# Eight attention heads beside a projection: the norm weights of queries and keys, four short steps and the score products change place and engine

## The chip, the cores and the metric

The kernel runs on one core of one Trainium2 chip. The metric is device time in microseconds of one execution, lower is better. The time given for a kernel is the median of its runs, and beside it stands one further execution that was profiled.

## What is computed

One layer of a streaming encoder, for 512 new frames of a prompt and 64 frames that continue a running stream with 512 cached positions (together 576 columns, called T in the kernel). All arithmetic is in float32. The part that matters here is the attention of eight heads:

```python
hn = rmsnorm(x, g_norm1)
proj = hn @ w_in                                     # 576 x 2048 by 2048 x 6144
q = rmsnorm(q.reshape(B, T, N_HEADS, HEAD_DIM), g_q) # per head, 128 wide
k = rmsnorm(k.reshape(B, T, N_HEADS, HEAD_DIM), g_k) # k, with g_k, is an output too
z = einsum(q, k) / sqrt(HEAD_DIM)                    # scores
log_1mb = where(mask, log_sigmoid(-z), 0)
after = reversed cumulative sum of log_1mb over keys, without the key itself
w = where(mask, exp(log_sigmoid(z) + after), 0)
o_attn = w @ v
```

Around it stand a short gated convolution, an output projection, and a feed-forward block, which the change leaves as they are.

## The kernel before

**Precision.** A float32 matrix is split into a high part in a reduced format and a low part (the rest), and a product is three matmuls: high by high, low by high, high by low. The high part is a copy on ScalarE (`cast`, L728; for weights L206), the low part a subtraction on VectorE (`low`, L731; for weights L209). Three subtractions of a head run on GpSimd instead (`low_pool`, L742): `s1l`, `s0l` and `vl`.

**Stages.** The program first loads and turns x, then runs some projections as block products ("units", PE line L1038, until about 162 us of the profile), then the last twelve column blocks of the input projection one after the other (PE line L247, tile `pj`; called the late projection here), then the convolution, the output projection and the feed-forward block (L1389, L1901). The attention of the eight heads is woven into the late projection and the first of the convolution, from about 163 to 441 us.

**What sets the order.** A small class `Pipeline` counts ticks. One tick is one step of a product, three matmuls of `pj`. `attend(h)` is a generator; it says `yield until(n)` to be called again n ticks after its start, and head h starts 49 ticks after head h-1. Whatever it issues then goes, in that order, into the queues of all engines. In this stage TensorE (PE), VectorE (DVE), ScalarE (ACT), GpSimd (POOL) and the DMA queue of SyncE (SP) all keep the program's order, so an instruction that waits holds up all that stands behind it on its engine. A head takes 104 ticks and the next starts after 49: two heads are always under way, and what I call the *frame* of head h (ticks counted from its start) also holds the second half of head h-1.

**One head, in ticks of its frame (before).** At 0 the raw queries and keys (`Eq`, `Ek`) and the cached keys `cK` are loaded; at 9 and 11 ScalarE squares them (L778) and at 12 VectorE sums the squares (L781). At 18 PE adds the sums over partitions (`ss`, L788), and ScalarE and VectorE make the factor 1/rms from them (L790 to L797). At 21 VectorE multiplies keys, then queries, by that factor, and GpSimd multiplies each by its norm weights (L800, L801). At 25 and 27 VectorE turns them into `kf` and `qf` (L804, L807), ScalarE makes the high parts `kh`, `qh`, VectorE the low parts `kl`, `ql` (28 and 30). The finished keys go out to HBM at 28 (`put_tokens`, eight DMAs, L716). From 36 to 41 PE computes the scores `z` (L832, L835). ScalarE and VectorE make softplus values `pr`, their high and low parts `ph` and `pl`, and the sums `s1`, `s0`. At 60, 63 and 66 PE adds the cumulative sums into `z` (L893 to L912), after each VectorE limits it (L883) and ScalarE takes the exponent (L885) and the high part again. At 67 and 69 the values get their parts `vh`, `vl`. At 78 PE multiplies weights and values (`po`, L937, L940). From 70 on the same follows for the 64 columns of the running stream (`sp`, `cz` at 87, `os` at 99).

**Weights.** Each block of weights (1 MB) has one place in memory: its two ScalarE copies stand 7 ticks after the start of each block of 32 ticks, its two VectorE subtractions `wlo` at 9 and 11, and the load of the block after it at 16, which waits for these subtractions. So these fall at another place of the frame in each head: in the frames of heads 1, 3 and 5 both subtractions stand between `ss` and the scores.

Of the kernel before, what the change touches and what calls it, by code (L numbers as in the profile page):

```python
# [16 lines left out]
P = 128  # L17
# [81 lines left out]
def tile_hybrid_stream_step(  # L99
# [26 lines left out]
    small = rpad.tile([P, 88], F32, name="rpad_t")  # L126
    NB = T // 32
    eps_r, gk_t, quad = small[:, :NB], small[:, NB : NB + 32], small[:, NB + 32 : NB + 36]
    gq_t = small[:, 56:88]
# [179 lines left out]
    def load_vectors():  # L309
        r0 = 0  # L310
        for name, ap, n in (("gq", g_q[0], 1), ("gk", g_k[0], 1),
                            ("ga", g_attn_out[0], NH), ("gc", g_conv_out[0], NG),
                            ("cw", conv_w[0].rearrange("w d -> (w d)"), 3 * NG),
                            ("st", state_conv[0, 0].rearrange("w d -> (w d)"), 2 * NG), ("g2", g_norm2[0], KD)):
            rows[name] = r0
            nc.sync.dma_start(out=vraw[r0 : r0 + n, :], in_=ap.rearrange("(r c) -> r c", c=P))
            r0 += n
        for q in range(4):
            nc.sync.dma_start(out=gk_t[32 * q : 32 * (q + 1), :],
                              in_=g_k[0, 32 * q : 32 * (q + 1)].partition_broadcast(32))  # L320
            nc.sync.dma_start(out=gq_t[32 * q : 32 * (q + 1), :],
                              in_=g_q[0, 32 * q : 32 * (q + 1)].partition_broadcast(32))

    g1c = const.tile([P, KD], F32, name="g1c")
    vec = const.tile([P, P], F32, name="vec")

    def turn_vectors():
# [3 lines left out]
        nc.vector.tensor_scalar(out=gq_t, in0=gq_t, scalar1=1.0 / math.sqrt(P), scalar2=None, op0=ALU.mult)  # L331
# [7 lines left out]
    def col(name, i=0):  # L339
        return vec[:, rows[name] + i : rows[name] + i + 1]  # L340
# [386 lines left out]
    def cast(hi, src):  # L727
        nc.scalar.copy(out=hi, in_=src)  # L728
# [12 lines left out]
    def low_pool(lo, src, hi):  # L741
        nc.gpsimd.tensor_tensor(out=lo, in0=src, in1=hi.bitcast(F32), op=ALU.subtract)  # L742

    late_E = {}

    def attend(h):
        clock = [0]

        def until(t):
            d, clock[0] = t - clock[0], t  # L750
            assert d >= 0
            return d
# [4 lines left out]
        for n, c in (("q", 0), ("k", 1)):  # L757
            if (c, h) in late_E:
                E[n] = late_E[c, h]
            else:  # L760
                E[n] = t1.tile([P, T], F32, tag="E" + n, name="E" + n)
                nc.sync.dma_start(out=E[n], in_=qk_dram[2 * h + c])
        cK = t1.tile([P, TP], F32, tag="cK", name="cK")
# [3 lines left out]

        def chunks(t, w=32):
            return t.rearrange("p (b c) -> p b c", c=w)

# [8 lines left out]
        yield until(12)  # L779
# [6 lines left out]
        yield until(18)  # L786
# [7 lines left out]
        yield until(21)  # L794
# [3 lines left out]
        for i, (n, g) in enumerate((("k", gk_t), ("q", gq_t))):  # L798
            r = ms[:, NB * (1 - i) : NB * (2 - i)].unsqueeze(2).to_broadcast([P, NB, 32])
            nc.vector.tensor_tensor(out=chunks(E[n]), in0=chunks(E[n]), in1=r, op=ALU.mult)  # L800
            nc.gpsimd.tensor_tensor(out=chunks(E[n]), in0=chunks(E[n]),  # L801
                                    in1=g.unsqueeze(1).to_broadcast([P, NB, 32]), op=ALU.mult)
            yield until(23 + 2 * i)
        nc.vector.transpose(out=kf, in_=E["k"])  # L804
        cast(kh, kf[:, : 3 * P])
        yield until(27)
        nc.vector.transpose(out=qf, in_=E["q"])  # L807
# [32 lines left out]
        yield until(38)  # L840
        scores(1)
        soft_log(pr[1], z[1][:, :384])
        yield until(39)
# [3 lines left out]
        yield until(41)  # L847
# [5 lines left out]
        yield until(43)  # L853
# [6 lines left out]
        yield until(44)  # L860
# [3 lines left out]
        yield until(46)  # L864
# [5 lines left out]
        yield until(48)  # L870
        low_pool(s1l, pb[2], s1h)
        cast(s0h, pb[1])
        yield until(50)
        cast(ph[0], pb[0])
        low_pool(s0l, pb[1], s0h)
        if h != 7:
            load_values(h)
        yield until(52)
# [9 lines left out]
        yield until(56)  # L888
        if h == 7:
            load_values(h)  # L890
        vtok = vtoks.pop(h)
        yield until(60)
# [5 lines left out]
        yield until(63)  # L898
# [5 lines left out]
        yield until(64)  # L904
# [3 lines left out]
        yield until(66)  # L908
# [5 lines left out]
        yield until(67)  # L914
# [4 lines left out]
        yield until(69)  # L919
        low_pool(vl, vtok[:, 0:3, :], vh)  # L920
# [3 lines left out]
        yield until(70)  # L924
        sp = scratch[:, 1280 : 1280 + T]
        soft_log(sp[:, :320], zc)
        yield until(73)
# [7 lines left out]
        yield until(78)  # L935
# [5 lines left out]
        yield until(79)  # L941
# [4 lines left out]
        yield until(81)  # L946
# [3 lines left out]
        yield until(87)  # L950
# [8 lines left out]
        yield until(88)  # L959
        nc.scalar.activation(out=ws[:, TS:], in_=ws[:, TS:], func=AF.Exp)  # L960
        yield until(99)
# [5 lines left out]
        for i, (a, b) in enumerate(HALVES):  # L967
            yield until(101 + 2 * i)
            add_squares(acc_a[:, a:b], o_attn[h][:, a:b], h == 0, scratch[:, HALF * i : HALF * (i + 1)])
# [195 lines left out]
    for q in (2, 3):  # L1165
        pipe.spawn(unit_prepare(*horder[q]))
# [1084 lines left out]
```

## Time and profile before

| | us |
|---|---|
| median of 3 runs (lowest, highest) | 2370.11 (2366.62, 2373.37) |
| the profiled execution, its own time | 2372.08 |
| its span, first to last instruction | 2370.3 |
| PE busy | 2334.1 |
| DVE busy | 1907.4 |
| ACT busy | 1150.0 |
| POOL busy | 315.0 |

The profiled execution lies 2.0 us above the median and inside the three runs. In rows of the profile, `out<-in` are the tiles that an instruction writes and reads, and "idle before" is the time that its engine stood still just before it, with the instruction whose end released it. A granted clock (PEclk) of 0.50 means that TensorE ran at half rate in that stretch.

### The profile page before, as it was taken

To read this page: it belongs to the slowest core of one execution; us is meant where nothing else is said; L and a number is where in the kernel's file an instruction comes from. 1 tells how busy PE (TensorE), PEld (TensorE's weight loads), DVE (VectorE), ACT (ScalarE), POOL (GpSimd) and SP (SyncE) were. 2 spreads that over 40 slices of the span, in tenths; PEclk is the share of its full clock that TensorE was granted. 3 is DMA by queue.
4 is the path that set the end of the run, shared out by engine and by line. 5 is a ranking of instruction groups with operands and counts; after the bars stand their busy time and mean duration, and the time that the engine had idled before them with its cause. 6 is when DMAs were issued, how large, how long until landed. Compare 5 with 4: busy or idle time off the path is not lost.

```text
span 2370.3 us, 43741 instructions
## 1 busy us (share of the span) xinstructions
PE 2334.1 (98%) x17461; PEld 2320.3 (98%) x17461; DVE 1907.4 (80%) x2817; ACT 1150.0 (49%) x1994; POOL 315.0 (13%) x424
## 2 busy tenths in 40 slices
PE   8999999999999999999999999999999999999999
PEld 8998898999999999999999999999999999999998
DVE  8876667688887889888888888888888777887886
ACT  7536666444444555444444444444444444444444
POOL 2003544212111220000000000000000001431121
PEclk9999999999999999999999999999999999999999
DMA  8785455784468655554554554554554946885654
GB/s 274 200 226 136 114 125 116 231 271 120 125 213 238 180 160 167 147 144 134 147 146 133 147 147 133 146 148 132 146 149 133 339 133 197 228 236 190 197 127 105
DMA packets 584836, 401.97 MB, mean 170 GB/s; under 512 B 92030, under 2 KB 572024, under 8 KB 584632
## 3 DMA queue, kind: packets, MB, share of 16 engines
q1 hardware_dynamic: 573704, 378.03, 54.6%
q0 software_dynamic: 10064, 20.65, 3.9%
q8 instruction: 137, 2.24, 0.4%
q10 hardware_dynamic: 864, 0.49, 0.1%
q14 instruction: 67, 0.55, 0.1%
HBM read 303.25 MB, written 95.86 MB: 168 GB/s over the span
## 4 chain that ended last, share of the span: by engine, by line
PE 79%; DVE 8%; DMA 5%; issue 3%; ACT 2%; SPq 1%; POOL 1%; DVEq 0%; ACTq 0%; POOLq 0%
PE psy L1901 34%; PE psw L1901 17%; PE psx L1901 8%; PE psy L1389 6%; PE pj L247 3%; PE psw L1389 3%; PE psy L1038 2%; DMA raw_a<-in_w_in_dram 2%; PE psx L1389 1%; PE psw L1038 1%; DMA Eq<-qk_dram 1%; DVE wlo L209 1%; DMA raw_a<-in_w_down_dram 1%; PE psx L1038 1%; PE pjo L247 1%
## 5 line engine op out<-in xcount | busy, mean ns | idle before, releaser
L1901 PE MATMUL psy<-h_s,whl 128*128 128x288 f32 x2787 | 411.6, 295 | 0.8 <-DMA h_s<-hid_dram 0.6
L1901 PEld LDWEIGHTS psy<-h_s,whl 128*128 128x128 f32 x2787 | 383.4, 188 | 1.3 <-DMA h_s<-hid_dram 0.8
L257 DVE TENSOR_TENSOR whl<-raw_a,whl 128x1024 fp32r<-128x1024 f32 (+4 forms) x296 | 316.8, 1071 | 60.1 <-ACT whl L256 58.9
L1901 PE MATMUL psw<-t,whl 128*128 128x288 f32 x2400 | 347.2, 295 | 0.0
L1901 PEld LDWEIGHTS psw<-t,whl 128*128 128x128 f32 x2400 | 327.3, 188 | 0.3 <-DVE whl L257 0.2
L256 ACT CAST whl<-raw_a 128x1024 fp32r<-128x1024 f32 (+4 forms) x296 | 268.1, 907 | 108.4 <-issue 35.4
L247 PE MATMUL pj<-x,whi 128*128 128x288 f32 x1376 | 298.0, 301 | 0.4 <-DVE x L408 0.2
L257 DVE TENSOR_TENSOR whl<-raw_b,whl 128x1024 fp32r<-128x1024 f32 (+5 forms) x190 | 197.5, 1040 | 69.4 <-ACT whl L256 68.2
L256 ACT CAST whl<-raw_b 128x1024 fp32r<-128x1024 f32 (+5 forms) x190 | 165.0, 871 | 168.9 <-issue 73.0
L1911 ACT COPY part<-psy 128x288 f32<-128x288 f32 x242 | 96.4, 398 | 279.5 <-PE psy L1901 276.7
L247 PEld LDWEIGHTS pj<-x,whi 128*128 128x128 f32 x1376 | 229.9, 191 | 2.1 <-DVE x L408 1.1
L247 PE MATMUL pj<-x,wlo 128*128 128x288 f32 x688 | 204.8, 298 | 0.1
L1901 PE MATMUL psy<-t2t,whl 128*128 128x288 f32 x1212 | 183.7, 295 | 0.0
L1901 PE MATMUL psy<-b22m,whl 128*128 128x288 f32 x1212 | 183.3, 295 | 0.0
L1901 PE MATMUL psx<-h_s,whl 128*128 128x288 f32 x1185 | 173.6, 295 | 0.0
L1901 PEld LDWEIGHTS psy<-t2t,whl 128*128 128x128 f32 x1212 | 168.3, 188 | 0.2 <-DVE whl L257 0.2
L1901 PEld LDWEIGHTS psy<-b22m,whl 128*128 128x128 f32 x1212 | 168.0, 188 | 0.0
L1901 PEld LDWEIGHTS psx<-h_s,whl 128*128 128x128 f32 x1185 | 162.3, 188 | 0.0
L247 PEld LDWEIGHTS pj<-x,wlo 128*128 128x128 f32 x688 | 132.2, 192 | 1.1 <-DVE wlo L475 0.3
L1680 POOL DMA_DIRECT2D hid_dram<-form x3 | 2.3, 755 | 970.4 <-DVE form L257 970.4
L256 ACT CAST whl<-s 128x1024 fp32r<-128x1024 f32 (+5 forms) x81 | 72.2, 892 | 99.9 <-PE psw L1901 99.8
L1901 PE MATMUL psy<-t,whl 128*128 128x288 f32 x576 | 107.5, 296 | 1.9 <-ACT part L1911 1.9
(534 smaller groups left out, 4527.0 us busy)
## 6 DMA issues: line engine op xcount, KB each, us to landing
hid_dram<-form SPq DMA_DIRECT2D x147, 288.0 KB, 2.6
raw_a<-in_w_in_dram SPq DMA_DIRECT2D x33, 1024.0 KB, 6.1
raw_a<-in_w_gate_dram SPq DMA_DIRECT2D x22, 1024.0 KB, 5.8
raw_a<-in_w_up_dram SPq DMA_DIRECT2D x22, 1024.0 KB, 5.8
raw_b<-in_w_gate_dram SPq DMA_DIRECT2D x22, 1024.0 KB, 8.3
raw_b<-in_w_up_dram SPq DMA_DIRECT2D x22, 1024.0 KB, 7.3
h_s<-hid_dram SPq DMA_DIRECT2D x10, 2016.0 KB, 12.8
raw_a<-in_w_out_dram SPq DMA_DIRECT2D x16, 1024.0 KB, 5.8
```

Source lines behind the costliest of these rows:

```text
L209: nc.vector.tensor_tensor(out=lo[:, a : a + 1024], in0=raw[:, a : a + 1024], in1=hi[:, a : a + 1024].bitcast(F32), op=ALU.subtract)
L247: mm(ps, w_[:, k, csl], x_, start=(k == 0 and n == 0), stop=(k == nk - 1 and n == 2))
L256: nc.scalar.copy(out=hi, in_=src)
L257: (lo_eng or nc.vector).tensor_tensor(out=lo, in0=src, in1=hi.bitcast(F32), op=ALU.subtract)
L1038: mm(ps, whl[:, w_, j, :], x_, start=(start and j == 0 and q == 0), stop=(j == NP - 1 and q == 2), skip_group_check=True)
L1389: mm(ps, whl[:, w_, j, :], x_, start=(start and j == 0 and q == 0), stop=(j == m - 1 and q == 2), skip_group_check=True)
L1680: q.dma_start(out=hid_dram[fp][2 * n - 2 : 2 * n].rearrange("f p t -> p f t"), in_=t.bitcast(F32))
L1901: mm(ps, whl[:, w_, j, :], x_, start=(start and j == 0 and q == 0), stop=(j == len(xs_) - 1 and q == 2), skip_group_check=True)
L1911: nc.scalar.copy(out=t, in_=st["y"])
```

## The change

For each head:

- The norm weights are multiplied in after the turn, by ScalarE, as the per-partition scale of a copy in place: `gqs` (query weights by 1/sqrt(128)) for `qf`, the column of `g_k` for `kf`, 128x576 each. GpSimd's two multiplications before the turn go; one of them comes back behind the turn of the keys, for the key output alone.
- VectorE now takes queries first, then keys, and turns each right after its product with 1/rms.
- `s1l`, `s0l` and `vl` are subtracted on VectorE; `low_pool` is gone.
- Later ticks: `cK` is loaded at 6 instead of 0, the sums stand at 13 (12), `ss` at 20 (18), the key output at 35 (28), the scores at 46 (36), and all behind them ten ticks later, but for `cz`, which is eleven later. The head's last step is at 113.
- Head 7 loads its values like the others, at 60.
- Outside the heads, the fourth preparation of unit weights starts 3 ticks after the third instead of with it, and the broadcast copy of `g_q` with its four DMAs is gone.

```diff
-        yield until(18)
+        yield until(20)
         ss = misc("ss")[:, : 2 * NB]
         mm(ss, same, sums, start=True, stop=True)
...
-        for i, (n, g) in enumerate((("k", gk_t), ("q", gq_t))):
-            r = ms[:, NB * (1 - i) : NB * (2 - i)].unsqueeze(2).to_broadcast([P, NB, 32])
+        for i, n in enumerate("qk"):
+            r = ms[:, NB * i : NB * (i + 1)].unsqueeze(2).to_broadcast([P, NB, 32])
             nc.vector.tensor_tensor(out=chunks(E[n]), in0=chunks(E[n]), in1=r, op=ALU.mult)
-            nc.gpsimd.tensor_tensor(out=chunks(E[n]), in0=chunks(E[n]),
-                                    in1=g.unsqueeze(1).to_broadcast([P, NB, 32]), op=ALU.mult)
-            yield until(23 + 2 * i)
-        nc.vector.transpose(out=kf, in_=E["k"])
+            yield until(25 + 2 * i)
+            nc.vector.transpose(out=f[n], in_=E[n])
+        nc.gpsimd.tensor_tensor(out=chunks(E["k"]), in0=chunks(E["k"]),
+                                in1=gk_t.unsqueeze(1).to_broadcast([P, NB, 32]), op=ALU.mult)
+        yield until(28)
+        nc.scalar.activation(out=qf, in_=qf, func=AF.Copy, scale=gqs)
+        cast(qh, qf[:, :TP])
+        yield until(30)
+        nc.scalar.activation(out=kf, in_=kf, func=AF.Copy, scale=col("gk"))
         cast(kh, kf[:, : 3 * P])
-        yield until(27)
-        nc.vector.transpose(out=qf, in_=E["q"])
-        cast(qh, qf[:, :TP])
-        yield until(28)
+        yield until(31)
+        low(ql, qf[:, :TP], qh)
+        yield until(33)
         low(kl, kf[:, : 3 * P], kh)
+        yield until(35)
+        nc.vector.transpose(out=cK, in_=cK)
         put_tokens(E["k"], kp[:, h, :], 0, TP)
         put_tokens(E["k"], ks[:, h, :], TP, T)
-        yield until(30)
-        low(ql, qf[:, :TP], qh)
-        yield until(31)
-        nc.vector.transpose(out=cK, in_=cK)
-        yield until(36)
+        yield until(46)
...
-        low_pool(s1l, pb[2], s1h)
+        low(s1l, pb[2], s1h)
...
-        low_pool(s0l, pb[1], s0h)
+        low(s0l, pb[1], s0h)
...
-        low_pool(vl, vtok[:, 0:3, :], vh)
+        low(vl, vtok[:, 0:3, :], vh)
...
-        pipe.spawn(unit_prepare(*horder[q]))
+        pipe.spawn(unit_prepare(*horder[q]), 3 * (q - 2))
```

VectorE in the frame of head 3, between the factor 1/rms and the scores, before. `wlo` are the weight subtractions, `z`, `pl`, `vl` belong to head 2, the rest to head 3; `raw_a` 128x36 is the factor.

```order
L796 TENSOR_TENSOR raw_a<-raw_a 128x36
L797 SCALAR_TENSOR_TENSOR raw_a<-raw_a 128x36
L800 TENSOR_TENSOR Ek<-Ek,raw_a 128x576
L209 TENSOR_TENSOR wlo_3214<-raw_a,whi_3213 128x1024
L800 TENSOR_TENSOR Eq<-Eq,raw_a 128x576
L739 SCALAR_TENSOR_TENSOR raw_a<-raw_a 128x320
L209 TENSOR_TENSOR wlo_3214<-raw_a,whi_3213 128x1024
L804 STREAM_TRANSPOSE kf<-Ek 128x576
L807 STREAM_TRANSPOSE qf<-Eq 128x576
L731 TENSOR_TENSOR kl<-kf,kh 128x384
L1120 STREAM_TRANSPOSE El<-pj 128x288
L731 TENSOR_TENSOR ql<-qf,qh 128x512
```

The same place of the same frame now, from a limit `z` behind the product of `Eq` on (the first weight subtraction, the factor and that product stand ahead of these rows).

```order
L880 SCALAR_TENSOR_TENSOR z_3004<-z_3004,acA 128x128
L208 TENSOR_TENSOR wlo_3180<-raw_a,whi_3179 128x1024
L798 STREAM_TRANSPOSE qf<-Eq 128x576
L796 TENSOR_TENSOR Ek<-Ek,raw_a 128x576
L730 TENSOR_TENSOR pl_3014<-pr_3008,ph_3011 128x256
L798 STREAM_TRANSPOSE kf<-Ek 128x576
L880 SCALAR_TENSOR_TENSOR z_3003<-z_3003,acA 128x128
L730 TENSOR_TENSOR pl_3013<-pr_3007,ph_3010 128x384
L1114 STREAM_TRANSPOSE El<-pj 128x288
L730 TENSOR_TENSOR vl<-vtok,vh 128x384
L730 TENSOR_TENSOR pl_3012<-pr_3006,ph_3009 128x512
L730 TENSOR_TENSOR ql<-qf,qh 128x512
```

What moved: head 2's limits `z`, its `pl` and its `vl` now stand among head 3's products, turns and subtractions; before, they stood ahead of them (and `vl` on GpSimd).

ScalarE in the frame of head 3, before: the last exponent and high part of head 2, the factor's logarithm and exponent (L792, L793), `vh`, the weights' copies, the softplus of head 2's stream columns (L734 to L736), then the high parts of head 3.

```order
L885 ACTIVATE pr_2966<-z_2963 128x512
L728 CAST ph_2969<-pr_2966 128x512
L792 ACTIVATE raw_a<-raw_a 128x36
L793 ACTIVATE raw_a<-raw_a 128x36
L728 CAST vh<-vtok 128x384
L206 CAST whi_3213<-raw_a 128x1024 x2
L734 ACTIVATE raw_a<-raw_a 128x320
L735 ACTIVATE raw_a<-raw_a 128x320
L736 ACTIVATE raw_a<-raw_a 128x320
L728 CAST kh<-kf 128x384
L728 CAST qh<-qf 128x512
```

The same on ScalarE now:

```order
L205 CAST whi_3179<-raw_a 128x1024 x2
L788 ACTIVATE raw_a<-raw_a 128x36
L789 ACTIVATE raw_a<-raw_a 128x36
L882 ACTIVATE pr_3008<-z_3005 128x384
L727 CAST ph_3011<-pr_3008 128x256
L882 ACTIVATE pr_3007<-z_3004 128x384
L727 CAST ph_3010<-pr_3007 128x384
L882 ACTIVATE pr_3006<-z_3003 128x512
L727 CAST ph_3009<-pr_3006 128x512
L802 ACTIVATE qf<-qf,gqs 128x576
L727 CAST qh<-qf 128x512
L727 CAST vh<-vtok 128x384
```

What moved: the factor now comes ahead of head 2's three exponents instead of behind them, and `vh` stands behind head 3's new copy of `qf` and behind `qh`; the copy of `kf` and `kh` follow it.

VectorE at the start of the unit products (around 77 us of the profile), before. `whl<-raw_a` is the low part of the third unit's weights, `own` a sum for the fourth unit, `xf` and `xr` other work.

```order
L1012 TENSOR_TENSOR own<-raw_a,raw_g 128x1024
L257 TENSOR_TENSOR xf_588<-xr_1068,xf_588 128x288
L731 TENSOR_TENSOR whl<-raw_a,whl 128x1024
L257 TENSOR_TENSOR xf_590<-xr_1070,xf_590 128x288
L731 TENSOR_TENSOR whl<-raw_a,whl 128x1024
```

And now:

```order
L256 TENSOR_TENSOR xf_585<-xr_1065,xf_585 128x288
L730 TENSOR_TENSOR whl<-raw_a,whl 128x1024
L256 TENSOR_TENSOR xf_587<-xr_1067,xf_587 128x288
L1006 TENSOR_TENSOR own<-raw_a,raw_g 128x1024
L730 TENSOR_TENSOR whl<-raw_a,whl 128x1024
```

The sum `own` moved from ahead of the third unit's low part to behind it.

More of the change, by code (lines that the diff above doesn't have):

```diff
@@ L125, in tile_hybrid_stream_step @@
     rpad = ctx.enter_context(tc.tile_pool(name="rpad", bufs=1, side="right"))
-    small = rpad.tile([P, 88], F32, name="rpad_t")
+    small = rpad.tile([P, 56], F32, name="rpad_t")
     NB = T // 32
     eps_r, gk_t, quad = small[:, :NB], small[:, NB : NB + 32], small[:, NB + 32 : NB + 36]
-    gq_t = small[:, 56:88]
     acon = tc.alloc_tile_pool(name="acon", bufs=1, side="left")
@@ L330, in turn_vectors @@
         nc.vector.tensor_copy(vec, ps[:, :P])
-        nc.vector.tensor_scalar(out=gq_t, in0=gq_t, scalar1=1.0 / math.sqrt(P), scalar2=None, op0=ALU.mult)
+        nc.vector.tensor_scalar(out=gqs, in0=vec[:, rows["gq"] : rows["gq"] + 1], scalar1=1.0 / math.sqrt(P),
+                                scalar2=None, op0=ALU.mult)
     nhalf = const.tile([P, 5], F32, name="nhalf")
```

68 lines of the change are left out of this document (31 added, 37 removed).

## The prediction

> **What bounds the kernel now.** The page first: TensorE is busy for 2334.1 us of this span.
>
> ```profile
> span 2370.3 us, 43741 instructions
> ```
>
> So the question is what TensorE loses where the change acts. The list of its waits, cut to 60 to 480 us, gives that (total, times, longest):
>
> ```profile
> PE z L835 <- ACT qh L728: 12.9, 7, 3.6
> PE ss L788 <- DVE raw_a L781: 3.7, 2, 2.4
> PE z L835 <- DVE ql L731: 2.0, 5, 0.7
> PE psy L1038 <- DVE whl L731: 1.2, 1, 1.2
> PE po L940 <- POOL vl L742: 1.0, 2, 0.7
> ```
>
> Four of these rows belong to the heads, 12.9 + 3.7 + 2.0 + 1.0 = 19.6 us; the fourth row, 1.2, is the start of the unit products. Two thirds of it is one place: the scores wait for `qh`. The windows add what a total of waits hides (PE busy comes first, the granted clock stands behind POOL):
>
> ```profile
> 172.90:176.30 3.40, 3.40 (x16) 3.40 (x16) 2.29 (x7) 0.47 (x2) 1.31 (x2) 0.50 1.10 294
> 213.90:217.30 3.40, 3.18 (x13) 3.18 (x14) 1.79 (x4) 2.03 (x4) 0.73 (x2) 0.50 1.13 310
> 275.30:282.10 6.80, 5.36 (x20) 5.06 (x21) 4.53 (x10) 3.88 (x8) 1.95 (x5) 0.50 0.87 258
> 340.20:347.00 6.80, 6.27 (x24) 6.05 (x25) 3.65 (x7) 4.25 (x9) 2.43 (x6) 0.50 0.61 134
> ```
>
> TensorE works at half rate in four stretches, and each stands at a long wait. Busy time there is 3.40 + 3.18 + 5.36 + 6.27 = 18.2 us, half of which, 9.1, full clock would save. So at most 19.6 + 9.1 = 28.7 us can be won in the heads.
>
> The timeline of TensorE shows waits with and without that sequel:
>
> ```profile
> 172.65 0.41 PE L788 MATMUL ss<-raw_a,acA 128*128 128x36 f32 x2 [2.36 <-DVE raw_a L781]
> ...
> 200.44 0.38 PE L788 MATMUL ss<-raw_a,acA 128*128 128x36 f32 x2 [1.37 <-DVE raw_a L781]
> ...
> 276.75 0.58 PE L835 MATMUL z<-qh,kh 128*128 128x256 f32 x1 [3.35 <-ACT qh L728]
> ```
>
> The 2.36 was followed by 3.4 us at half rate, the 3.35 lies at the start of 6.8, and the 1.37 had no such stretch behind it. I therefore price a wait of 2.2 us or more at itself plus 3.4 / 2 = 1.7 us, and a shorter one at itself.
>
> Why the scores are late shows on VectorE, in the frame of head 3:
>
> ```profile
> 264.46 0.18 DVE L790 SCALAR_TENSOR_TENSOR raw_a<-ss,rpad_t 128x36 f32<-128x36 f32 x1
> ...
> 266.34 0.69 DVE L731 TENSOR_TENSOR pl<-pr,ph 128x512 fp32r<-128x512 f32 x1 [0.59 <-ACT ph L728]
> ...
> 268.34 0.76 DVE L800 TENSOR_TENSOR Ek<-Ek,raw_a 128x576 f32<-128x576 f32 x1
> 269.01 1.22 DVE L209 TENSOR_TENSOR wlo<-raw_a,whi 128x1024 fp32r<-128x1024 f32 x1
> 270.15 1.78 DVE L800 TENSOR_TENSOR Eq<-Eq,raw_a 128x576 f32<-128x576 f32 x1
> ...
> 272.26 2.43 DVE L209 TENSOR_TENSOR wlo<-raw_a,whi 128x1024 fp32r<-128x1024 f32 x1
> 274.62 0.77 DVE L804 STREAM_TRANSPOSE kf<-Ek 128x576 f32<-128x576 f32 x1
> 275.31 0.73 DVE L807 STREAM_TRANSPOSE qf<-Eq 128x576 f32<-128x576 f32 x1
> 275.97 0.55 DVE L731 TENSOR_TENSOR kl<-kf,kh 128x384 fp32r<-128x384 f32 x1
> ...
> 276.83 0.65 DVE L731 TENSOR_TENSOR ql<-qf,qh 128x512 fp32r<-128x512 f32 x1
> ```
>
> From the factor to the turn of the queries VectorE never stands still: two weight subtractions lie between, and beside GpSimd's product one of them took 2.43 us instead of 1.22, and the product of `Eq` 1.78 instead of 0.76. Starts of neighbours are closer than the durations say; taken from starts, a subtraction `wlo` costs 1.14, a product 0.67, a turn 0.69.
>
> **The change part by part.** One tick is 0.395 us, and between the first cumulative sum (tick 11 of the frame) and `ss` (18) lie 4.86 us:
>
> ```profile
> 163.13 0.29 PE L247 MATMUL pj<-x,wlo 128*128 128x288 f32 x1
> 163.52 0.30 PE L247 MATMUL pj<-x,wlo 128*128 128x288 f32 x1
> ...
> 259.24 0.38 PE L893 MATMUL z<-pr,acA 128*128 128x128 f32 x2
> ...
> 264.10 0.31 PE L788 MATMUL ss<-raw_a,acA 128*128 128x36 f32 x2
> ```
>
> Seven ticks are 2.77, so the three blocks of cumulative sums take 2.09 us of TensorE. Before, they stood ahead of `ss`; now they stand behind it, in ticks 21 to 27.
>
> *Scores.* They come 26 ticks behind `ss` instead of 18, with these blocks and with `po` in between: 26 × 0.395 + 2.1 + 1.7 (`po`) + 0.1 = 14.1 us after it. I lay VectorE's new order for head 3 end to end from `ss` at 0: `ms` by 0.4; the limit of block 2, which TensorE ends at 1.5, by 2.2; `wlo` by 3.2; three short steps by 3.9; product of queries by 4.6; limit 4.8; `wlo` 5.9; turn of queries 6.6; product of keys 7.3; `pl` 7.6; turn of keys 8.3; last limit 8.6. `qh` follows at 11.2, `ql` by some 13, `kl` at some 15. The scores would come at 14.1, and with the wait of `po` below at 16.3: they no longer wait. −14.9 us of waits (12.9 + 2.0).
>
> *`po`, the new latest.* TensorE reaches it 19 ticks behind `ss`: 19 × 0.395 + 2.1 + 0.1 = 9.7. It needs `vh` and `vl`, which now stand behind head 3's new copy and `qh`. Prices on ScalarE, and of `vl` before:
>
> ```profile
> 265.07 0.59 ACT L885 ACTIVATE pr<-z 128x512 f32<-128x512 f32 x1
> 265.69 0.62 ACT L728 CAST ph<-pr 128x512 fp32r<-128x512 f32 x1
> ...
> 266.61 0.50 ACT L728 CAST vh<-vtok 128x384 fp32r<-128x384 f32 x1
> ```
>
> ```profile
> L675 ACT ACTIVATE xsq<-xf,g1c x2: 532/534/536, 63.0 to 72.4; 128x288 f32<-128x288 f32 x2
> ```
>
> ```profile
> L778 ACT ACTIVATE qf<-Eq x8: 670/676/687, 168.5 to 385.4; 128x576 f32<-128x576 f32 x8
> ```
>
> ```profile
> 267.20 1.05 POOL L742 TENSOR_TENSOR vl<-vtok,vh 128x384 fp32r<-128x384 f32 x1 [2.38 <-ACT vh L728]
> ```
>
> The copy with a scale is not in the trace at 128x576. Bounds: the square of that size, 0.68, and twice the scaled copy of 288 columns, 1.07; I take 0.78, nearer to the square, since the size is the same. The last limit ends at 8.6; exponent to 9.3, `ph` 9.8, copy 10.6, `qh` 11.2, `vh` 11.7, `vl` on VectorE (0.55, as `kl`) 12.3. `po` would start its `vh` products 2.0 late and lose about 0.2 more at `vl`: 2.2 us. Laid out in the same way with the weights' copies and subtractions where they stand, frames 1 to 7 give 2.7, 0.1, 2.2, 0.1, 1.6, 0.5, 0.9, in all 8.1 against 1.0 before. The frames of 1 and 3 reach 2.2, so two stretches at half clock, 3.4.
>
> *`ss`.* Two ticks later, 0.8 us: head 0's wait falls from 2.36 to 1.6, head 1's to 0.3; in frames 2 and 4 subtractions of the other head now stand ahead of the sums, 0.7 and 1.5. Together 4.1 against 3.7.
>
> *`cz`*, one tick later relative to its head, but its low part is queued behind head 3's work: I put 0.5 in each of three even frames, 1.5, from 0 to 1 each.
>
> *Short subtractions.* VectorE gets three per head, 0.41 to 0.55 us each, about 1.5; it is busy for 1907 of 2370 us, and the cost above contains `vl`. `s1l` and `s0l` lie ten ticks (4 us) ahead of their use. What goes with GpSimd's two products is its hold on VectorE:
>
> ```profile
> 272.01 1.59 POOL L801 TENSOR_TENSOR Eq<-Eq,rpad_t 128x576 f32<-128x576 f32 x1 [0.70 <-DVE Eq L800]
> ```
>
> The key product that comes back on GpSimd is waited for by the key output alone.
>
> *Key output and loads.* The next head's loads of `Eq`, `Ek` stand behind the eight output DMAs in SP's queue:
>
> ```profile
> L716 SPq DMA_DIRECT2D out_dram<-Ek x64: 327/480/1138, 177.1 to 408.7; - x64
> ```
>
> ```profile
> DMA to landing us min/median/max: 6.4/6.6/8.6
> ```
>
> (The second row is that of the loads of `Eq`.) The output is issued from 10.5 on, 8 × 0.48 = 3.9 us; the load follows at 14.5 and lands at 21. The squares need it some 2.6 us ahead of the next `ss`, at about 27.4. Six us of cover: priced at nothing.
>
> *Unit start.* `own` no longer stands ahead of the weights that TensorE awaits:
>
> ```profile
> 80.16 0.40 PE L1038 MATMUL psy<-x,whl 128*128 128x288 f32 x1 [1.17 <-DVE whl L731]
> ```
>
> ```profile
> 77.38 1.22 DVE L1012 TENSOR_TENSOR own<-raw_a,raw_g 128x1024 f32<-128x1024 f32 x1
> 78.52 0.45 DVE L257 TENSOR_TENSOR xf<-xr,xf 128x288 fp32r<-128x288 f32 x1
> ```
>
> Start to start 1.14 of the 1.17: −1.1, between 0 (if the weights, not VectorE, are late) and −1.2. The four small DMAs of `g_q` and head 7's values: nothing waits for them in the list.
>
> **Sum.** Gone: 28.7. New: `po` 8.1, `ss` 4.1, `cz` 1.5, half clock 3.4, together 17.1. −28.7 + 17.1 − 1.1 = −12.7 us on the profiled 2372.1, that is 2359.4; the median lies 2.0 lower, so 2357.
>
> The Trainium skill, "TensorE: Matmul & The Clock Gate", section "HAM oscillation — how this bites in real kernels", states that it is idle gaps of TensorE above about 3.4 us that bring the clock down. This trace differs: the 2.36 us wait was enough. By the page none of my waits would cost clock and the sum would be 3.4 lower; the measurement decides, and I keep it.
>
> **The rivals.**
>
> - *`po` takes over whole.* The stall moves and keeps its size. If starts aren't closer than durations and the new copies cost 1.07, the same chains end later: 3.2, 3.2, 2.5, 1.9 in odd frames and 0.9, 0.9, 1.2 in even ones, 13.8; with `ss` 4.1, `cz` 1.5 and as much half clock as before, 9.1, that is 28.5 against 28.7. With the unit start −1.3: 2369. For it: in frame 3 a subtraction already took 2.43. Against: the partner on GpSimd goes.
> - *All stalls go but head 0's `ss`, 1.6:* −28.7 + 1.6 − 1.1 = −28.2, 2342. This holds if VectorE, free of GpSimd's products, runs about 2 us ahead of my laying out. Against: my order has no gap to close.
> - *Slower: the loads of the next head come late.* Place: SP's queue, where the output now waits for GpSimd's product behind the turn of the keys. If that takes over 6 us more than reckoned, `ss` waits in each of seven heads. Priced like head 0, 2.4 + 1.7 = 4.1 each: 7 × 4.1 = 28.4 on top of my sum, −12.7 + 28.4 = +15.7, 2386. For it: single key output DMAs took up to 1.14 us; against: the slack of six.
>
> **How the numbers follow.** My forecast gets 0.62, the first rival 0.18, the second 0.12, the slower one 0.08. Own range of the forecast: 2349 (`cz` and half clock nil, `po` 3 less) to 2365 (`po` 4 more with two more stretches of 1.7). The whole range, 2343 to 2369, leaves out the slower case and most of the outer half of the other two. About 0.3%, 7.1 us, can be told from no change here. Faster by more (below 2363): 0.57 of the forecast's chance and all of the second rival, 0.69; within: the first rival and 0.04 of the forecast, 0.22; slower: the third rival's 0.08 and 0.01 of the forecast, if `po` ends far later than the first rival says, 0.09.
>
> **What would show it.** Right: in TensorE's list the wait of `z L835` is nearly gone and `po` stands first with about 8 us, released by ScalarE's `vh` or VectorE's `vl`, above 2 us in the frames of heads 1 and 3; the half-clock stretches shrink to two; `whl` at 80 us is gone; copies of `qf`, `kf` take 0.7 to 0.9 us; no VectorE row of `wlo` in the heads is near 2.4. Wrong: scores still waiting for `kl`, `ss` waiting for a DMA of `Eq` or `Ek`, `po` with 13 us and four half-clock stretches, or hardly any wait at all.

## The result and the profile after

| | us |
|---|---|
| before, median of 4 runs (lowest, highest) | 2368.43 (2366.62, 2373.37) |
| changed, median of 4 runs (lowest, highest) | 2346.99 (2346.21, 2347.74) |
| ratio, 95% interval | 0.9906 (0.9889 to 0.9923) |
| profiled executions, spans | 2370.3 before, 2345.0 changed |

The changed kernel is faster by 0.9%, 21.4 us in the medians and 25.3 us between the two profiled spans. First the page of the changed kernel, span and first line:

```profile
span 2345.0 us, 43719 instructions
...
PE 2322.5 (99%) x17461; PEld 2311.2 (99%) x17461; DVE 1903.2 (81%) x2841; ACT 1162.6 (50%) x2010; POOL 281.8 (12%) x392
```

TensorE has as many matmuls as before (17461), and its busy time fell by 11.6 us, so part of the gain is work done faster and not waiting saved. TensorE's waits from 60 to 480 us, the list that answers to the prediction's first:

```profile
PE po L934 <- ACT vh L727: 4.3, 4, 1.8
PE ss L784 <- DVE raw_a L777: 1.8, 3, 1.1
PE cz L947 <- DVE spl L730: 1.1, 3, 0.4
PE po L934 <- DVE vl L730: 0.8, 4, 0.2
PE cz L946 <- ACT sph L727: 0.4, 1, 0.4
```

The scores (`z`) are gone from the list, and so is `whl` at 80 us. `po` is now the latest, released by `vh`. In all 8.4 us are left of 19.6. The stretch from 160 to 440 us of each profile, which the heads fill, before and then changed (PE busy first; the granted clock stands behind POOL):

```profile
160.00:440.00 280.00, 260.17 (x1841) 252.86 (x1841) 185.43 (x308) 161.51 (x321) 114.11 (x171) 0.96 0.51 127
```

```profile
160.00:440.00 280.00, 271.36 (x1982) 264.82 (x1981) 189.86 (x352) 183.40 (x356) 81.77 (x148) 1.00 0.54 147
```

The mean clock went from 0.96 to 1.00: the changed kernel has no stretch at half clock in the heads. What such a stretch costs can be read from one place, which the changed kernel runs at full clock:

```profile
172.90:176.30 3.40, 3.40 (x27) 3.40 (x27) 3.29 (x6) 2.31 (x4) 0.75 (x1) 1.00 0.38 124
```

27 matmuls stand where the prediction's row of before has 16: 40% is lost at half clock, a little less than the half that I reckoned with. On 18.2 us that is 7.4. (Two of the 16 are short matmuls of `ss`; the `pj` matmuls alone start 0.24 us apart there instead of 0.132, and on that the loss would be 8.2.)

The account of the profiled 25.3 us: waits in the heads 19.6 − 8.4 = 11.2; half clock 7.4; the start of the unit products 1.2; and some 5 us in the feed-forward, which no step of the prediction touched. That stretch, before and then changed:

```profile
1890.00:2330.00 440.00, 437.91 (x3290) 437.02 (x3290) 353.02 (x498) 190.63 (x328) 90.00 (x98) 1.00 0.65 188
```

```profile
1890.00:2330.00 440.00, 440.00 (x3330) 439.81 (x3329) 359.26 (x509) 194.89 (x342) 96.03 (x104) 1.00 0.61 182
```

In the same 440 us the changed kernel does 40 matmuls more; at one per 0.132 us (440 / 3330) that is 5.3 us. Only 2.1 us of it are waits of TensorE (440 − 437.91). The rest needs a cause of its own, which the last experiments look for. The four terms make 25.1.

The order of the matmuls gives a second account that needs no pricing, since every kernel here has the same number of them. I call the time from the start of the 1,200th to that of the 3,010th the *heads' stretch*; all matmuls of the eight heads lie in it, and it went from 276.0 to 257.5 us, 18.5 less (11.2 + 7.4 = 18.6 above). From the first matmul up to it the changed kernel gains 1.6, and behind it another 0.7 up to the 7,201st matmul (the kernel before has a fifth half-clock stretch there, at 524.5 us, which the account above leaves out); then it loses 0.7 up to the 13,001st, and it gains 5.8 in the rest.

### The profile page after: what moved, and what is told of

The parts are those of the page before. It is cut to its first block, busy times and chain, and to the rows that moved or that the text cites. A ratio compares the mean times of both kernels' runs of the same rounds, so it can differ in the third digit from the quotient of the medians.

```text
span 2345.0 us, 43719 instructions
## 1 busy us (share of the span) xinstructions
PE 2322.5 (99%) x17461; PEld 2311.2 (99%) x17461; DVE 1903.2 (81%) x2841; ACT 1162.6 (50%) x2010; POOL 281.8 (12%) x392
## 4 chain that ended last, share of the span: by engine, by line
PE 89%; DVE 5%; ACT 2%; DMA 2%; issue 1%; POOL 0%; SPq 0%; ACTq 0%; DVEq 0%; POOLq 0%
PE psy L1895 35%; PE psw L1895 18%; PE psx L1895 9%; PE psy L1383 6%; PE pj L246 6%; PE pjo L246 4%; PE psw L1383 3%; PE psy L1032 2%; PE psx L1383 1%; PE psw L1032 1%; DVE wlo L208 1%; DMA raw_a<-in_w_in_dram 1%; PE psx L1032 1%; PE po L934 0%; PE z L833 0%
## 6 DMA issues: line engine op xcount, KB each, us to landing
h_s<-hid_dram SPq DMA_DIRECT2D x10, 2016.0 KB, 11.6
```

## The experiments

Two questions led them: which part of the change gives the gain in the heads, and where the microseconds in the feed-forward come from. Each run is given with its median and its ratio to runs of the kernel before on the same chip.

### The change in two halves

The kernel before with the later ticks alone, every tick of a head from the scores on ten later:

```diff
-        yield until(36)
+        yield until(46)
...
-        yield until(99)
+        yield until(109)
```

> The kernel before, in which only the later ticks change: the scores at 46 instead of 36, all behind them ten later, cz and the exponent behind it at 97 and 98. Engines and order of queries and keys as before. Theory (room): the scores waited because TensorE came too early; from ss to the scores it is then 28 ticks x 0.395 + 2.1 (the cumulative sums, now behind ss) + 1.7 (po) = 15 us, and the old chain ends at 13 to 14. So the waits of the scores (14.9 us) nearly go, po waits 1 to 2.4 us in odd frames, waits of the heads 8 to 13 us instead of 19.6, at most one stretch at half clock: 2349 to 2356. Rival (engines): the chain with GpSimd's products in it is what is too long, and the ten ticks only put the limits and parts of the other head into it: scores or po wait 15 us or more, three or four half-clock stretches, 2362 to 2370.

Measured: 2367.21, ratio 0.9983 (0.9974 to 0.9993). TensorE's waits of that run:

```profile
PE po L940 <- ACT vh L728: 7.0, 5, 2.8
PE po L940 <- POOL vl L742: 5.7, 7, 0.9
PE ss L788 <- DVE raw_a L781: 2.1, 2, 1.7
```

The scores no longer wait, as the room theory had it, but `po` takes over with 12.7 us, more than the 1 to 2.4 per odd frame that I gave it, and three stretches at half clock remain in the heads. So the room theory is right on the scores and wrong on the rest: the time lies in the rival's range (2362 to 2370), with three half-clock stretches as the rival had it, and where it had 15 us of waits or more, there are 12.7. The heads' stretch is 8.1 us shorter than before; the median gains 4.1.

The changed kernel with the old later ticks, every tick from the scores on ten earlier:

```diff
-        yield until(46)
+        yield until(36)
...
-        yield until(109)
+        yield until(99)
```

> The changed kernel with the later ticks of before: scores at 36 again, all behind them ten earlier; the moves between engines, queries first, and ss at 20 stay. Theory (room): TensorE is at the scores 16 ticks x 0.395 + 1.7 (po) + 0.1 = 8.1 us after ss, and kh is ready at about 12 in odd frames: 3 to 4 us of wait there as before, 2 to 4 half-clock stretches, 2358 to 2368. Rival (engines): the shorter chain alone suffices, scores wait under 1 us each, no half clock, 2345 to 2352.

Measured: 2367.43, ratio 0.9986 (0.9977 to 0.9995). Its list:

```profile
PE z L833 <- DVE kl L730: 12.6, 8, 1.9
PE z L833 <- ACT kh L727: 8.4, 4, 3.0
```

The scores wait 21.0 us, more than the 14.9 before, now for the keys, which come second, and four stretches, seven windows of 3.4 us in all, run at half clock: this speaks for the room theory. The moves alone make the heads' stretch 3.0 us longer; the 4 us that the run's median gains lie outside it, at the start of the unit products and behind the heads. So in the heads' stretch the room alone gives 8.1 us, the moves alone lose 3.0, and both together give 18.5. They aren't two gains that add: with early scores the chain to `kl` is too long however it is cut, and with late scores and the old chain `po` starves behind the last exponent.

### Which part of the engine moves matters

Three runs undo one move each in the changed kernel. The norm weights back on GpSimd, ahead of the turns (with the tile of `gq_t`, as before):

```diff
+            nc.gpsimd.tensor_tensor(out=chunks(E[n]), in0=chunks(E[n]),
+                                    in1=g.unsqueeze(1).to_broadcast([P, NB, 32]), op=ALU.mult)
             yield until(25 + 2 * i)
             nc.vector.transpose(out=f[n], in_=E[n])
...
-        nc.scalar.activation(out=qf, in_=qf, func=AF.Copy, scale=gqs)
...
-        nc.scalar.activation(out=kf, in_=kf, func=AF.Copy, scale=col("gk"))
```

> The changed kernel with the norm weights back on GpSimd, ahead of the turns (queries first as now); ScalarE's two copies with a scale and the separate product for the key output go. Theory (the chain of VectorE to the last limit, exponent, qh, vh is what po waits for): in frame 3 the turn of the keys then waits for GpSimd's second product, the last limit ends at about 10.2 us after ss instead of 8.2; ScalarE saves 0.77 ahead of vh, so vh is 1.2 us later. Waits of po from 5.1 to about 10 us, two stretches at half clock, 2347 + 5 + 3.4 = 2355. Rival (GpSimd's products hide as the copies do): 2345 to 2349, waits of po at 5.

Measured: 2369.90, ratio 0.9998 (0.9988 to 1.0007): nothing is left of the gain in time; of the 18.5 us in the heads' stretch 4.8 are left. VectorE in the frame of head 3:

```profile
264.16 2.47 DVE L209 TENSOR_TENSOR wlo<-raw_a,whi 128x1024 fp32r<-128x1024 f32 x1
...
269.43 0.78 DVE L801 STREAM_TRANSPOSE kf<-Ek 128x576 f32<-128x576 f32 x1 [1.13 <-POOL Ek L798]
270.13 0.27 DVE L879 SCALAR_TENSOR_TENSOR z<-z,acA 128x128 f32<-128x128 f32 x1
```

Here is the cost twice over: the subtraction beside GpSimd's product takes 2.47 us where it takes 1.21 in the changed kernel, and then the turn waits 1.13 us for GpSimd's second product. The limit that the last exponent needs stands behind both. TensorE's `po` waits:

```profile
272.66 0.38 PE L933 MATMUL po<-ph,vh 128*128 128x256 f32 x1 [3.04 <-ACT vh L728]
```

The waits of `po` are 12.7 + 1.5 us against 5.1, with two half-clock stretches. The theory's mechanism holds, its size doesn't: it had 10 us, since it left out the even frames (0.9 to 1.0 each). The run lies 15 us over its forecast of 2355. `po` explains 4 of them and `ss` 1.7 (3.5 against 1.8); some 2 lie at the start of the convolution (waits of 2.06 and 0.86 us and a half-clock stretch), and nearly 5 in the feed-forward, for which the wide tile (below) accounts in part.

The three short subtractions back on GpSimd (`s1l` and `s0l` in the same way):

```diff
-        low(vl, vtok[:, 0:3, :], vh)
+        low_pool(vl, vtok[:, 0:3, :], vh)
```

> The changed kernel with s1l, s0l and vl back on GpSimd. Theory: s1l and s0l change nothing; vl takes about 1.0 us instead of 0.56 and lies at the end of the chain, so the wait of po at vl grows from 0.21 to 0.8 in each of seven frames (0.7 to 0.9 in the run with the ticks alone): +4.1 us, and frame 1 has 1.84 + 0.8 in one place, which brings one stretch at half clock, +1.7: 2353. Rival (VectorE's load is what counts: three subtractions less on it bring limits and turns forward): 2344 to 2348.

Measured: 2350.51, ratio 0.9917 (0.9902 to 0.9932), 3.5 us over the changed kernel. The wait of `po` at `vl` is 3.5 us in five frames (0.8 at most) against 0.8 in four, and two half-clock stretches come with it. The theory had 6 us and one stretch; VectorE's load, the rival, doesn't count.

Keys ahead of queries again, in the products and turns (shown) and then in the copies, high and low parts:

```diff
-        for i, n in enumerate("qk"):
+        for i, n in enumerate("kq"):
```

> The changed kernel with keys ahead of queries in products, turns, copies and low parts, as before. Theory (the order of the two carries nothing, the last limit and vh have the same work ahead of them): waits of the heads 7 to 9 us, 2346 to 2349. Rival (the order is part of the gain): ql is then last, the scores wait 0.5 us or more in each odd frame, and po is later: 2350 or more.

Measured: 2355.17, ratio 0.9934 (0.9919 to 0.9949): 8 us slower, so my theory fell. `po` waits 8.3 us, and three half-clock windows are back. But it isn't the rival's `ql` either. GpSimd's product for the key output starts as soon as the keys are turned, in the frame of head 1:

```profile
198.91 1.59 POOL L799 TENSOR_TENSOR Ek<-Ek,rpad_t 128x576 f32<-128x576 f32 x1 [5.01 <-DVE kf L798]
```

```profile
199.33 1.46 DVE L730 TENSOR_TENSOR pl<-pr,ph 128x256 fp32r<-128x256 f32 x1
```

VectorE's `pl`, a 0.41 us instruction, takes 1.46 beside it, and the last limit is behind `pl`. In the changed kernel the same product starts behind the start of that limit (201.94):

```profile
202.17 1.57 POOL L799 TENSOR_TENSOR Ek<-Ek,rpad_t 128x576 f32<-128x576 f32 x1 [7.82 <-DVE kf L798]
```

The frames agree: `pl` takes 1.46 in frames 1, 3 and 7, and there the wait of `po` for `vh` is longer than in the changed kernel by 0.94, 1.08 and 0.93 us; in frame 5 `pl` isn't stretched, and the wait is 0.60 against 0.57. The order matters by where GpSimd's product falls.

### `vh` earlier and later

`vh` ahead of the last exponent:

```diff
+        yield until(75)
+        cast(vh, vtok[:, 0:3, :])
         yield until(76)
...
         yield until(77)
+        low(vl, vtok[:, 0:3, :], vh)
         low(pl[1], pb[1], ph[1])
-        cast(vh, vtok[:, 0:3, :])
-        yield until(79)
-        low(vl, vtok[:, 0:3, :], vh)
```

> The changed kernel with vh at tick 75 (in the frame of the next head: 26) instead of 77, ahead of the last exponent and of the copy of qf and qh on ScalarE, and vl at 77 ahead of pl. Theory: the 5.1 us for which po waits come from vh standing behind three instructions that po does not need; they fall to under 1.5 us, and the time by 3 to 5 us against the changed kernel, to about 2343. Rival: po is then as late by pl or ph of the last block, or the scores by kl since TensorE comes earlier; waits of the heads stay at 7 to 9 us and the time at 2347.

Measured: 2343.00, ratio 0.9881 (0.9865 to 0.9897), 4 us faster than the changed kernel. Its list:

```profile
PE cz L948 <- DVE spl L730: 2.1, 6, 0.4
PE ss L784 <- DVE raw_a L777: 2.0, 3, 1.1
PE cz L947 <- ACT sph L727: 0.2, 1, 0.2
```

`po` is gone from it, and the scores didn't take its place: the theory holds as written.

`vh` behind the copy of `kf` and `kh`, the same step as a dose in the other direction:

```diff
         yield until(80)
+        cast(vh, vtok[:, 0:3, :])
+        low(vl, vtok[:, 0:3, :], vh)
```

> The changed kernel with vh and vl behind the copy of kf and kh (1.28 us more of ScalarE ahead of them). Dose for po and for the clock: waits of po at vh of 1.84, 1.25, 0.57, 0.65 us in frames 1, 3, 5, 7 grow by 1.3 each, to 3.1, 2.5, 1.9, 1.9, in all +5.2 us. Theory (a wait of 2.2 us or more is followed by a stretch at half clock): two such stretches of 3.4 us, +3.4 us more, 2347 + 8.6 = 2356. Rival (no wait here is long enough): granted clock 1.00 throughout, 2347 + 5.2 = 2352. The Trainium skill, TensorE: Matmul & The Clock Gate, HAM oscillation, puts the bound at about 3.4 us and so stands with the rival.

Measured: 2356.09, ratio 0.9939 (0.9924 to 0.9954), 9.1 us slower than the changed kernel (8.6 expected). Three waits of `po` on TensorE:

```profile
206.41 0.38 PE L934 MATMUL po<-ph,vh 128*128 128x256 f32 x1 [3.06 <-ACT vh L727]
...
269.02 0.38 PE L934 MATMUL po<-ph,vh 128*128 128x256 f32 x1 [2.46 <-ACT vh L727]
...
392.37 0.38 PE L934 MATMUL po<-ph,vh 128*128 128x256 f32 x1 [1.89 <-ACT vh L727]
```

```profile
207.90:211.30 3.40, 3.40 (x14) 3.11 (x13) 1.39 (x3) 1.26 (x2) 1.50 (x5) 0.50 0.54 136
269.34:272.75 3.41, 3.20 (x11) 2.85 (x11) 1.80 (x4) 1.01 (x4) 1.42 (x5) 0.50 0.37 64
```

Behind the first two stands a stretch at half clock, behind the third none. Waits well under 3.4 us cost clock here, as the prediction reckoned.

### The start of the unit products

```diff
-        pipe.spawn(unit_prepare(*horder[q]), 3 * (q - 2))
+        pipe.spawn(unit_prepare(*horder[q]))
```

> The changed kernel with the fourth preparation of unit weights started with the third, as before. Theory: own stands ahead of whl again, TensorE waits 1.2 us once at about 80 us, 2348. Rival (that wait came from the load of the weights or is not tied to own): no wait there, 2347.

Measured: 2348.23, ratio 0.9911 (0.9896 to 0.9926), which can't be told from the changed kernel; but the wait is back, 1.99 us:

```profile
81.02 0.40 PE L1032 MATMUL psy<-x,whl 128*128 128x288 f32 x1 [1.99 <-DVE whl L730]
```

### Two tries to go on

`vh` first, and `cz` and the exponent behind it two ticks later:

```diff
-        yield until(98)
+        yield until(100)
```

> The kernel with vh first, and cz with its exponent two ticks later (100). Theory: cz waited 0.38 us in six frames for the low part behind it in VectorE's queue; 0.8 us more covers that: -2 us against the kernel with vh first, 2341. Rival: the sums of the running stream are then late for os at 109, or the waits of cz move to the next step: 2343.

Measured: 2341.40, ratio 0.9876 (0.9860 to 0.9893), the lowest time of the study. `cz` doesn't wait any more; `ss` now waits 4.0 us instead of 2.0, and one half-clock stretch follows its longest wait, 1.9. The gain over `vh` first, 1.6 us, is within what the two kernels' runs scatter (2341.2 to 2343.7 and 2340.4 to 2342.3).

In addition `ss` at 22 in the even heads:

```diff
-        yield until(20)
+        yield until(20 if h % 2 else 22)
```

> The kernel with vh first and cz two ticks later, in which ss stands at 22 instead of 20 in the even heads. Theory: ss waited 1.0, 1.0 and 1.9 us in heads 0, 2 and 4, the last followed by a stretch at half clock; 0.8 us of ticks and 0.7 of the block of cumulative sums that then lies ahead of it (heads 2, 4) take 0.8 + 1.0 + 1.5 away and the clock's 1.7: 2341.4 - 5 = 2336.4. Rival: the factor, the turns and the last limit come 1.5 us later in even frames, and po waits for pl there, 1 us or more in three frames: 2340 or more.

Measured: 2343.16, ratio 0.9880 (0.9863 to 0.9896): no gain. `ss` is down to 0.7 us, `po` doesn't wait (the rival fails on that), but `cz` waits 3.6 us again, for the softplus of the stream columns that is now later. The stall moved on by one step; the heads' stretch is 252.9 us long against 252.5. (The profile of this run also has a half-clock stretch at 699.5 us, behind the heads, where the kernels don't differ.)

### The feed-forward

The changed kernel with the small constant tile as wide as before, and nothing else:

```diff
-    small = rpad.tile([P, 56], F32, name="rpad_t")
+    small = rpad.tile([P, 88], F32, name="rpad_t")
```

> The changed kernel with the small constant tile 88 columns wide again (the 32 columns of gq_t stay empty), so that memory lies as before and no instruction differs. Question: waits of 2.4 us in all behind 1880 us (loads of h_s, ScalarE's part) stand in the profile of before and not of the changed kernel; those at h_s stand in all three profiles with the wide tile and in none with the narrow one. Theory (chance of the execution): the same time as the changed kernel, 2347, no wait at h_s that is more than in other profiles. Rival (layout): waits of some 1 us for h_s return, with them 2 to 4 us: 2349 to 2351.

Measured: 2351.02, ratio 0.9916 (0.9901 to 0.9931); all its runs (2349.96 to 2352.77) lie above all four of the changed kernel. The sign that the rival named, waits for `h_s`, is absent, so that half of it fell. But the stretch of the feed-forward is slow again, without waits:

```profile
1890.00:2330.00 440.00, 439.72 (x3305) 439.46 (x3305) 355.93 (x503) 192.69 (x340) 97.56 (x104) 1.00 0.62 182
```

25 matmuls fewer than with the narrow tile are 3.3 us. (The heads' stretch is 1.4 us longer as well, where waits of 1.37 and 0.21 us were followed by a half-clock stretch; the instructions there are the same, so I put that down to where the waits fell in the clock's windows.) Most of it shows when one counts how many matmuls of this stretch start 137 to 150 ns after the one ahead (the mean is 132; in every kernel some 270 to 460 stand at 136 ns, so the count leaves these out):

| kernels | tile, columns | such matmuls |
|---|---|---|
| before, ticks alone, weights on GpSimd, wide tile | 88 | 283, 225, 288, 274 |
| changed, and the other eight with 56 | 56 | 7 to 30 |
| 64 empty columns (below) | 120 | 14 |

In the run with the wide tile these matmuls cost 2.0 us over 132 ns each, and another 0.7 lies in 33 that start 152 or 153 ns after the one ahead. (The next expectation counts from 136, takes in a part of those at 136 ns, and so speaks of about 50 and 300.)

A third width, 256 bytes more than the narrow one:

```diff
-    small = rpad.tile([P, 56], F32, name="rpad_t")
+    small = rpad.tile([P, 120], F32, name="rpad_t")
```

> The changed kernel with the small constant tile 120 columns wide, 64 empty; no instruction differs. With 88 columns the time was 4 us above that with 56: 1.3 us came about in the heads (one stretch at half clock), 3.6 in the feed-forward, where about 300 matmuls stood 136 to 150 ns apart instead of 132. Theory (where the tiles lie): 256 bytes more than with 56 columns; if it is a matter of steps of 256 bytes, the feed-forward is as with 56 columns, about 50 such matmuls, 2346 to 2348. Rival (any shift away from the narrow tile, or more memory): 200 or more such matmuls, 2350 or more. Third (neither, the execution's chance): as with 56 columns too, so that only a slow result speaks against chance.

Measured: 2348.60, ratio 0.9905 (0.9888 to 0.9921), and its stretch:

```profile
1890.00:2330.00 440.00, 440.00 (x3329) 439.74 (x3328) 357.65 (x505) 194.42 (x341) 95.36 (x104) 1.00 0.62 182
```

As with 56 columns. So it isn't the amount of memory nor any shift as such: 88 columns are 128 bytes more than 56, 120 columns 256 bytes more, and only the first is slow. The times alone wouldn't settle it: the ratios with 56, 88 and 120 columns are 0.9906, 0.9916 and 0.9905, with intervals that overlap, and the 2348.60 lies a little above the theory's range. The profiled execution of this run is 4.2 us longer than the changed kernel's, but not in the feed-forward: 3.1 of it lie behind the heads and ahead of 1000 us, where TensorE waits for `whl`. What shows the width is the pace of these matmuls, slow in all four profiles with 88 columns and in none of the other ten; which tiles have to lie how, and why, stays open and wasn't tried.

## Why the prediction was right or wrong

The forecast of 2357 had the direction and, in the heads, the mechanism. The measured 2347 is 10 us lower: the whole range (2343 to 2369) holds it, the forecast's own range (2349 to 2365) doesn't. Between the profiled executions −12.7 was forecast and −25.3 measured. By its steps:

- **Scores: right.** No wait of `z` is left (−14.9 us forecast, and seen). The two halves show why it needs both: room alone moves the stall to `po`, the moves alone leave the scores waiting 21 us.
- **`po` becomes the latest: right, too large.** 8.1 us were forecast, 5.1 measured. Frame 3, which the prediction laid out from `ss` at 0, can be checked row by row; `ss` is at 253.59 on TensorE:

```profile
253.59 0.31 PE L784 MATMUL ss<-raw_a,acA 128*128 128x36 f32 x2
...
263.52 0.38 PE L931 MATMUL po<-pr,vtok 128*128 128x128 f32 x2
265.15 0.39 PE L934 MATMUL po<-ph,vh 128*128 128x256 f32 x1 [1.25 <-ACT vh L727]
265.74 0.39 PE L934 MATMUL po<-ph,vl 128*128 128x256 f32 x1 [0.21 <-DVE vl L730]
```

```profile
257.44 0.76 DVE L796 TENSOR_TENSOR Eq<-Eq,raw_a 128x576 f32<-128x576 f32 x1
...
261.81 0.27 DVE L880 SCALAR_TENSOR_TENSOR z<-z,acA 128x128 f32<-128x128 f32 x1
```

```profile
262.11 0.60 ACT L882 ACTIVATE pr<-z 128x512 f32<-128x512 f32 x1 [2.63 <-DVE z L880]
262.74 0.62 ACT L727 CAST ph<-pr 128x512 fp32r<-128x512 f32 x1
263.27 0.77 ACT L802 ACTIVATE qf<-qf,gqs 128x576 f32<-128x576 f32 x1
264.07 0.62 ACT L727 CAST qh<-qf 128x512 fp32r<-128x512 f32 x1
264.59 0.51 ACT L727 CAST vh<-vtok 128x384 fp32r<-128x384 f32 x1
```

  The last limit ended 8.5 us after `ss` (forecast 8.6), `vh` 11.5 (11.7); the scaled copy took 0.77 (0.78). TensorE came to `po` at 9.9 (9.7), and then did the two products with the raw values first, 0.4 us that I had left out because they need no `vh`. So the wait is 1.25 + 0.21 where I had 2.2. Frames 1, 3, 5, 7 gave 2.0, 1.5, 0.8, 0.9 (2.7, 2.2, 1.6, 0.9). With 0.7 less in frames 1 and 3, no frame came over the edge of the clock, and **the 3.4 us of half clock fell away with it**: the largest single step from a small error. Part of that is luck: the 2.0 us of frame 1 fell on both sides of a window's end (1.30 and 0.75 us; the windows are told of in the last section), and of the four profiles with these same instructions in the heads one, that with the wide tile, has a half-clock stretch.
- **`ss`: 4.1 forecast, 1.8 measured.** Head 0 waited 0.54 instead of 1.6, heads 2 and 4 0.19 and 1.11 instead of 0.7 and 1.5. The 0.3 that I gave to head 1 (two ticks off its 1.37 would have been 0.6) didn't come at all. Head 0's isn't a constant of the program: it was 0.4 to 1.5 in the profiles of kernels that don't differ up to there.
- **`cz`: right,** 1.5 us in three frames.
- **Unit start: right,** −1.2, and the run that undoes it has the wait back.
- **GpSimd's hold on VectorE: right, and understated.** It was named as a thing that goes, with no price. The weights' run shows that with the ticks in place it is worth 13.7 of the 18.5 us in the heads' stretch (that run saves ScalarE's two copies, too).
- **The unquestioned step: "The four small DMAs of `g_q` … nothing waits for them".** That is so, but the 32 columns that went with them change where other tiles lie, and some 260 matmuls of the feed-forward are no longer slowed: 3.3 us in the run that widens the tile alone. I priced the instructions of an edit and not the places of the tiles behind it. The rest of the feed-forward's gain, some 2 us, goes with waits in the profile of before, 1.9 us of them for ScalarE's `part`, of which the run with the wide tile alone has 0.3; what they come from stays open. For the forecast this part of the gain, 5.3 us in all, is luck: no step of the prediction touches it.

The 12.6 us that the sum missed are then: stalls sized too large, 3.0 (`po`) + 2.3 (`ss`) + 3.4 (clock); the half clock of before sized too large, 7.4 and not 9.1, −1.7; the feed-forward, 5.3; together 12.3. Of the rivals, the second (all stalls go but head 0's, 2342) came nearer in time than the forecast, 5 us off against 10, but not by its mechanism: 8.4 us of stalls remained, in the places that the forecast named. The first didn't come, nor the late loads of the slower one: `ss` waits for VectorE's sums only.

## What to carry to other kernels

When a stall is moved by giving its consumer more time, lay out the next consumer in the same queue as well; here the room alone gained 8.1 us in the heads' stretch, the shorter chain alone lost 3.0, and both together gained 18.5. Look for what a slow neighbour stretches: an output that nobody waits for (GpSimd's key product) cost 8 us, half clock included, where it fell beside VectorE's chain, and nothing that shows a few microseconds later. And a change to a small tile shifts whatever lies behind it: if a far stage changes its pace, test the width alone.

## What the runs showed of the hardware

**The clock goes down by windows of 3.41 us, not by the length of one wait.** In the profile of before the four stretches begin at 172.93, 213.88, 275.32 and 340.18 us, 12.0, 18.0 and 19.0 times 3.413 us apart, and their lengths are one or two such steps; the fifth, at 524.50, is 54.0 steps behind the fourth. The Trainium skill, "TensorE: Matmul & The Clock Gate", section "What's actually happening", gives a free-running window of 3413 ns; this trace agrees. What decides is how much of one window is idle. In the run with the ticks alone two waits followed each other on TensorE, neither long:

```profile
334.25 0.38 PE L940 MATMUL po<-ph,vh 128*128 128x256 f32 x1 [1.35 <-ACT vh L728]
...
335.43 0.58 PE L940 MATMUL po<-ph,vl 128*128 128x256 f32 x1 [0.79 <-POOL vl L742]
```

A half-clock stretch began at 334.96, behind a window with 1.68 us of idle time, while the wait of 1.89 us in the run with `vh` last, parted by a window's end (1.74 us inside), had none behind it. All fourteen profiles can be laid on this grid. From 60 to 2330 us and at full clock, windows with up to 1.55 us of idle time were never followed by half clock, those with 1.93 or more always (17 of them), and in between, from 1.58 to 1.89, eight were and seven were not: about half a window. At half clock the bound was lower: a window with 0.46 us of idle time or less was followed by full clock, one with 0.55 or more by another at half. The same page of the Trainium skill, section "HAM oscillation — how this bites in real kernels", warns of gaps above about 3.4 us; the measurement is stricter than that, and decides. The prediction's rule, 2.2 us or more in one wait, was near enough for its rows, but the wait isn't what counts.

**A VectorE instruction that starts while GpSimd's product is under way ends late.** 128x1024 took 2.47 and 1.21 us, 128x256 took 1.46 and 0.41, the longer ones beside a 128x576 product on GpSimd. In the run with keys first five `pl` of 128x256 began inside that product, and each ended 0.28 us behind it; in the weights' run three `wlo` of 128x1024 did, and each ended 1.08 us behind it. So they look like instructions that first waited for GpSimd's to end, not like instructions at a slower pace. In the same two runs 35 such instructions were already under way when a product of GpSimd began, and none of them was stretched (`Eq` in the run with keys first took its usual 0.72 us). At two places of the changed kernel the two start within 0.02 us of each other, and VectorE's took its usual 0.54.
